# Seven half-size products for the second merge gate, and a changed finish of the attention outputs

## The chip, the cores and the metric

The kernel runs on one core of one Trainium2 chip. A core has a matrix engine (TensorE, PE in the profile), a vector engine (VectorE, DVE), a scalar engine (ScalarE, ACT), a general engine (GpSimd, POOL) and a queue that only issues transfers here (SyncE, SP). Each executes its own list of instructions in order and waits for the others by semaphores. The metric is the device time of one execution in microseconds. Before the change it is 1616.22 us, the median of three runs (1616.01 to 1618.52).

## The reference

One layer of a gated backbone over 1024 latent tokens of width 1024, with 256 context tokens. Both branches start from one input projection of the normalised, modulated input `h`:

```python
p = h @ w_in                       # 11 column groups; the last two are m_gla and m_diff
# branch A: bidirectional chunked gated linear attention -> o_gla
# branch B: differential attention, 8 heads, softmax(q1 k1) - lam * softmax(q2 k2) over 1280 keys -> o_diff
a = merge_heads(rms_norm(o_gla) * gla_gain) * silu(gla_gate)
b = merge_heads(rms_norm(o_diff) * diff_gain * (1 - lam_init)) * silu(diff_gate)
y = sigmoid(m_gla) * (a @ w_br_gla) + sigmoid(m_diff) * (b @ w_br_diff)
x = x + g_x * (y @ w_out)
```

The change touches two things. One is the product that gives `m_diff`, 1024 tokens by 1024 inputs by 1024 channels, called the second merge gate here. The other is what happens to `o_diff` between the attention and the product with `w_br_diff`: the RMS norm over a head's 128 channels and the product with the gate (`diff_gain` and the gate's SiLU are in the stored gate already).

## The kernel before

**Arithmetic.** All large products take fp32 operands as two parts, hi and lo, in a reduced format. `mm3` issues three matmuls for each 128-row piece of the contraction (hi by hi, hi by lo, lo by hi), each with 128 stationary columns and up to 512 moving ones. A weight tile is split by ACT (copy to hi) and DVE (subtraction for lo).

**Order.** The kernel text is written as tasks, Python generators with priorities. When the kernel is built, a planner (`Driver`) runs the tasks against a model of the engines, with costs and latencies, and thereby fixes the order of instructions of every engine. A smaller number is the higher priority. On the chip each engine follows that order.

**Stages.** From 0 to about 890 us: normalisation, projections (four of them by seven half-size products per group, whose input sums `s1` to `s4` are kept in DRAM as `d_s`), and the linear attention. From about 900 to 1440 us: the differential attention, and in it a filler. From 1440 us: `diff`, the product with `w_br_diff`, and the output product.

**The attention.** Its unit is one head and 128 queries; there are 64. For each unit PE computes the scores of two components (12 matmuls into the PSUM tile `s`), DVE takes the maxima (`att_max`), ACT the exponentials (`att_exp`), DVE combines the two (`att_mix`, tile `e`), PE transposes the result in ten pieces (`ident,e`), and `att_split` makes hi and lo: for the first two groups of four pieces ACT copies to `ac` and POOL makes `at` hi and lo, for the last group of two ACT and DVE do it. Two units make a pair; `att_av` multiplies the pair by the values (30 matmuls with 256 columns, `at,vv`). `att_order` fixes the sequence of scores (S), transposes (T) and value products (A), scores some four units ahead of the value products. `att_fin` then finishes a pair: it copies the product, transposes it, forms the norm on ACT, DVE and POOL, multiplies, transposes back and stores to `d_bT`. There are 32 such finishes.

**The filler.** `fill` has the lowest priority (9) and puts its matmuls wherever the attention leaves PE free. It goes through a list: rows 6 and 7 of the first merge gate, the eight rows of the second, and the eight rows of `a @ w_br_gla` ("br"). A row is a weight of 1024 by 128, two slots of `wt` (four in all) for its hi and lo, loaded through `raw` (three slots of 512 KB). It gives two half tiles of 24 matmuls each in the PSUM tile `mb`, of which there is one. A gate's half tile ends in a tanh on ACT (`post`) and a store to `d_m`; a br half tile ends in one operation on DVE and a store to `d_y`. The moving operand of the gates is `hx`, the split input, which fills the 32 slots of `h0` and `h1`; when the gates are done, `d_aT` is loaded there for br. `pace` holds a half tile back until a given attention unit. `presums_a` forms sums of `w_br_diff` on POOL during the attention, in the four slots of `xa`.

**Queues.** All transfers are issued by SP, in the planner's order; a transfer whose source or slot isn't ready holds the ones behind it.

## Time and profile before

| | |
|---|---|
| time of the runs | 1616.22 us median, 1616.01 to 1618.52 |
| profiled execution | span 1614.1 us from first to last instruction; no other time of it is given, and the median lies 2.1 us above its span |
| busy share of the span | PE 99%, PE weight load 82%, DVE 76%, ACT 52%, POOL 39% |
| granted TensorE clock | 1.000 |
| attention and filler | about 900 to 1440 us |
| transfers | 331.16 MB, all compute transfers in one hardware queue |

The page gives totals, a strip of 40 slices, and groups of instructions by engine and operands (`out<-in`, buffer numbers left out). A busy PE is an engine with a matmul in its pipeline: one matmul's duration overlaps that of the next, so what one costs is read from how many fit into a stretch of time, not from its duration.

### The profile page before, as it was taken

The numbers are of one execution on the slowest core, as the hardware profiler recorded it, in microseconds if no ns is written. First come the engines' busy times: TensorE is split into PE (matmuls) and PEld (weight loads), VectorE is DVE, ScalarE is ACT, GpSimd is POOL, SyncE is SP. The second block draws the span as 40 slices with busy tenths as digits, with TensorE's granted clock in tenths as the row PEclk, the third lists the DMA queues.
The fourth block names the chain that finished last, engine by engine and source line by source line (L and its number), as shares of the span: only waits on it lengthen the run. The fifth ranks groups of instructions, "written<-read, shape, count | busy, mean of one in ns | idle before, by whom it ended". The sixth has DMA issues, their size and how long they took to land.

```text
span 1614.1 us, 24349 instructions
## 1 busy us (share of the span) xinstructions
PE 1591.4 (99%) x8229; PEld 1328.1 (82%) x8229; DVE 1224.4 (76%) x2118; ACT 835.7 (52%) x1720; POOL 634.3 (39%) x663
## 2 busy tenths in 40 slices
PE   8999999999999999999999999999999999999999
PEld 3788888888888888888888788888888888888887
DVE  4787945676777779767677688878778888888994
ACT  4776523435343454555535566665665666656331
POOL 1500000001415667535564256656765666560000
PEclk9999999999999999999999999999999999999999
DMA  8576996998878367564645944545587545347662
GB/s 305 201 257 239 329 304 232 344 331 295 278 238 281 116 194 235 167 212 118 189 118 158 253 121 121 151 129 151 150 264 218 159 137 150 111 155 285 204 206 100
DMA packets 259565, 331.16 MB, mean 205 GB/s; under 512 B 22600, under 2 KB 160752, under 8 KB 259440
## 3 DMA queue, kind: packets, MB, share of 16 engines
q1 hardware_dynamic: 259440, 329.60, 63.8%
q8 instruction: 65, 1.06, 0.3%
q14 instruction: 60, 0.49, 0.1%
HBM read 225.20 MB, written 104.33 MB: 204 GB/s over the span
## 4 chain that ended last, share of the span: by engine, by line
PE 89%; DVE 4%; issue 2%; DMA 2%; ACT 1%; POOL 1%; SPq 0%; ACTq 0%; DVEq 0%; POOLq 0%
PE mm L349 30%; PE mb L349 11%; PE s L349 8%; PE mc L349 7%; PE b L349 6%; PE tp L349 5%; PE gt L349 5%; PE b L375 5%; PE go L349 4%; PE gs L349 4%; PE mz L349 2%; PE tp L375 2%; DVE sm L201 1%; POOL at L201 1%; DMA w<-in_w_ada 1%
## 5 line engine op out<-in xcount | busy, mean ns | idle before, releaser
L349 PE MATMUL mm<-w,h 128*128 128x512 f32 x912 | 231.0, 400 | 0.0
L349 PE MATMUL mb<-h,wt 128*128 128x512 f32 x840 | 223.0, 400 | 0.0
L201 DVE TENSOR_REDUCE sm<-s 128x1 f32<-128x1024 f32 (+1 forms) x192 | 193.3, 1037 | 10.7 <-PE s L349 6.6
L201 ACT ACTIVATE e<-s,sm 128x1280 f32<-128x1280 f32 x128 | 169.3, 1329 | 54.4 <-DVE sm L201 51.2
L349 PEld LDWEIGHTS mm<-w,h 128*128 128x128 f32 x912 | 167.4, 188 | 32.8
L201 POOL TENSOR_TENSOR at<-ac,at 128x512 fp32r<-128x512 f32 x128 | 188.2, 1471 | 10.7
L349 PEld LDWEIGHTS mb<-h,wt 128*128 128x128 f32 x840 | 151.4, 188 | 28.6 <-DVE ft L201 0.3
L201 POOL TENSOR_SCALAR at<-ac 128x512 fp32r<-128x512 f32 x128 | 96.9, 757 | 191.0 <-ACT ac L201 190.7
L349 PE MATMUL s<-hk,aq 128*128 128x512 f32 x744 | 169.0, 363 | 1.9 <-ACT e L201 1.8
L349 PE MATMUL mm<-h,w 128*128 128x512 f32 x672 | 168.2, 400 | 1.0 <-DVE h L201 1.0
L349 PEld LDWEIGHTS mm<-h,w 128*128 128x128 f32 x672 | 123.7, 188 | 26.4 <-DVE h L201 1.5
L201 DVE TENSOR_TENSOR w<-raw,w 128x512 fp32r<-128x512 f32 x128 | 96.0, 766 | 54.2 <-ACT w L201 52.0
L349 PEld LDWEIGHTS s<-hk,aq 128*128 128x128 f32 x744 | 117.7, 189 | 18.5 <-ACT e L201 3.6
L349 PE MATMUL b<-at,vv 128*128 128x256 f32 x960 | 130.1, 287 | 1.1 <-ACT ac L201 0.8
L349 PEld LDWEIGHTS b<-at,vv 128*128 128x128 f32 x960 | 119.5, 191 | 2.8 <-ACT ac L201 1.0
L201 ACT ACTIVATE w<-raw 128x512 fp32r<-128x512 f32 x128 | 78.1, 626 | 84.2 <-PE tp L349 23.8
L201 ACT ACTIVATE ac<-b 128x512 f32<-128x512 f32 x122 | 72.5, 598 | 91.8 <-PE b L375 91.7
L201 POOL TENSOR_TENSOR sm<-sm,nhalf 128x2 f32<-128x2 f32 (+2 forms) x94 | 107.7, 1146 | 27.9 <-DVE sm L201 22.7
L201 DVE SCALAR_TENSOR_TENSOR e<-e,sm,e 128x1280 f32<-128x1280 f32 x64 | 117.9, 1842 | 1.0
L349 PE MATMUL mm<-w,g 128*128 128x512 f32 x432 | 105.7, 389 | 0.0
L349 PEld LDWEIGHTS mm<-w,g 128*128 128x128 f32 x432 | 81.1, 188 | 16.9
L375 PE MATMUL b<-ident,e 128*128 128x128 f32 x610 | 92.6, 273 | 1.3 <-ACT ac L201 0.8
(357 smaller groups left out, 3054.2 us busy)
## 6 DMA issues: line engine op xcount, KB each, us to landing
raw<-in_w_in SPq DMA_DIRECT2D x62, 512.0 KB, 4.3
g<-d_s SPq DMA_DIRECT2D x32, 640.0 KB, 6.2
g<-d_s SPq DMA_DIRECT2D x32, 512.0 KB, 5.7
aq<-d_qT SPq DMA_DIRECT2D x124, 128.0 KB, 3.4
d_dv<-pl SPq DMA_DIRECT2D x40, 256.0 KB, 3.9
gv<-d_v SPq DMA_DIRECT2D x40, 256.0 KB, 3.3
d_kT<-pl SPq DMA_DIRECT2D x40, 256.0 KB, 2.8
hk<-d_kT SPq DMA_DIRECT2D x32, 320.0 KB, 5.9
```

What stands on the lines that cost most here:

```text
L201: self.ins = f(out, *args, **kw).ins
L349: self.ins = self.nc.tensor.matmul(out, lhsT, rhs, start=start, stop=stop, skip_group_check=more).ins
L375: self.nc.tensor.transpose(out, src, self.ident[:n, :n])
```

## The change

The second merge gate is computed as a 2 by 2 block product by seven products of half size in every dimension (Winograd's form): `w11`, `w21` and `w22` with parts of the input, and four sums of weight blocks, `t1` to `t4`, with the input sums `s1` to `s4`. The input sums are read from `d_s`. For each of the seven products there are four tiles of 12 matmuls. Two of the products add into the PSUM tile of another (`w21` behind `w11`, `t4` behind `t3`).

The weight blocks are loaded as 512 rows by 256 columns into `raw`, 512 KB each; for `t1` to `t4` one to three more blocks are loaded and added or subtracted on POOL (14 operations of 128x1024). A `wt` slot holds hi and lo of one 512x128 block. Results that are needed again are kept in the four `xa` slots and in four freed slots of `h0` (`u5`), by a copy on ACT or an addition on DVE, and end in a tanh and a store as before. Slots of `h0` and `h1` go to the sums, and then to `d_aT`, piece by piece. `presums_a` starts only when the gate is done (`ev_md`), later than before.

In `att_fin` ACT copies the transposed output out of PSUM and squares it from there, the two small operations on each pair of statistics become one, and the product with the gate and with the norm become one DVE operation per unit. `z` of two units lies in one tile. `PP`, the priority of the fill's results, goes from -1 to -3.5.

```diff
@@ att_scores
+                if qt % 2 == 0:
+                    zp = self.t("sm", [P, 2, 2])
                 u = dict(hd=hd, qt=qt, ...
-                         z=self.t("sm", [P, 2]), left=2, ev=[Event() for _ in range(3)])
+                         z=zp[:, qt % 2], zp=zp, left=2, ev=[Event() for _ in range(3)])
@@
-    PM, PS, PF, PP = -2, -3, -2, -1
+    PM, PS, PF, PP = -2, -3, -2, -3.5
@@ att_fin
-        for x in range(2):
-            self.dve.tensor_scalar(z2[:, x:x + 1], zs[x][:, 0:1], zs[x][:, 0:1], EPS, ALU.mult, ALU.mult)
+        self.dve.scalar_tensor_tensor(z2, zp[:, :, 0], EPS, zp[:, :, 0], ALU.mult, ALU.mult)
...
+        oc = self.t("b1k", [P, 2, P])
+        ss = self.t("sm", [P, 2])
+        self.rel("b1", self.act.activation(oc, pt, AF.Copy))
+        for x in range(2):
+            e = self.act.activation(ot[:, x], oc[:, x], AF.Square, accum_out=ss[:, x:x + 1])
         self.rel("b1k", e)
-        yield On(e, "ACT")
-        oo = self.t("b1k", [P, 2, P])
-        ss = self.t("sm", [P, 2])
+        yield On(e, "DVE")
+        self.dve.scalar_tensor_tensor(ss, ss, 1.0 / P, z2, ALU.mult, ALU.add)
+        yield d.on("POOL", ss)
+        yield On(max(self.pool.tensor_tensor(ss, ss, self.nhalf[:, 0:2], ALU.pow), d.when(g)), "DVE")
         for x in range(2):
-            e = self.act.activation(oo[:, x], pt[:, x], AF.Square, accum_out=ss[:, x:x + 1])
-        yield d.on("DVE", pt, g)
-        e2 = self.dve.tensor_tensor(g, pt, g, ALU.mult)
-        self.rel("b1", max(e, e2))
-        yield On(e, "DVE")
-        for x in range(2):
-            self.dve.tensor_scalar(ss[:, x:x + 1], ss[:, x:x + 1], 1.0 / P, z2[:, x:x + 1], ALU.mult, ALU.add)
-        yield d.on("POOL", ss)
-        yield On(self.pool.tensor_tensor(ss, ss, self.nhalf[:, 0:2], ALU.pow), "DVE")
-        for x in range(2):
-            e = self.dve.tensor_scalar(oo[:, x], g[:, x], ss[:, x:x + 1], None, ALU.mult)
+            e = self.dve.scalar_tensor_tensor(oc[:, x], oc[:, x], ss[:, x:x + 1], g[:, x], ALU.mult, ALU.mult)
@@ fill
-        todo = [(0, s, self.win, C_MG + s * P) for s in range(self.fill_from, 16)] + \
-               [(1, s, a["w_br_gla"][0], s * P) for s in range(8)]
+        OPS = [(n, t) for t in (0, 2) for n in ("w11", "w21")] + [(n, t) for n in ("t2", "t1", "w22") for t in (0, 2)] + \
+              [(n, t) for t in (0, 2) for n in ("t3", "t4")]
+        gates, outs = range(self.fill_from, 8), range(8)
+        todo = [("mg", s) for s in gates] + [("md", n, t) for n, t in OPS] + [("br", s) for s in outs]
+        SUM = dict(t1=("w12", ("w11", ALU.subtract)), t3=("w22", ("w12", ALU.subtract)),
+                   t2=("w11", ("w22", ALU.add), ("w12", ALU.subtract)),
+                   t4=("w21", ("w11", ALU.subtract), ("w22", ALU.subtract), ("w12", ALU.add)))
...
+            for ev, f in parts:
+                yield ev
+                yield d.on("POOL", raw, ev.raw)
+                self.rel("raw", self.pool.tensor_tensor(raw, raw, ev.raw, f))
...
+        h0 = sums("s1") + [("u5",)] + sums("s3") + loads(0, 0, 1, 6, 7) + loads(1, 0, 1, 2, 3)
+        h1 = sums("s2") + sums("s4") + loads(0, 2, 3, 4, 5) + loads(1, 4, 5, 6, 7)
...
+        for t in range(4):
+            yield pace(i)
+            tg, pm = yield from new()
+            yield ev_op["w11", t]
+            yield from product(pm, "w11", t, (0, 0), True, True, copy(pm, X[t], ev_x[t]))
+            i += 0.5
+            yield ev_x[t]
+            e = yield from product(pm, "w21", t, (0, 4), False, True, direct(pm, t, tg))
+            i += 0.5
...
+        for t in range(4):
+            yield pace(i)
+            tg, pm = yield from new()
+            x = ev_u5.x[t]
+            yield from product(pm, "t3", t, "s3", True, True, plus(pm, x, x, ev_z[t], None, gate(x, 1, t, 1, ("h0", 1))))
+            i += 0.5
+            yield ev_z[t]
+            e = yield from product(pm, "t4", t, (1, 4), False, True,
+                                   plus(pm, X[t], X[t], Event(), tg, gate(X[t], 0, t, 1, ("xa", 1))))
+            i += 0.5
+        self.rel("h0", e, 8)
+        self.rel("h1", e, 8)
+        d.set(self.ev_md)
@@ presums_a
         yield self.ev_sb
+        yield self.ev_md
 
         def op(n, k, o, x, y, f, i):
-            yield self.ev_u[min(63, 3*i+9)]
+            yield self.ev_u[min(63, 28 + 2 * i)]
```

The planner's new order shows at three places. The first is PE around the 33rd of the 64 attention units. Before, filler matmuls (`mb<-h,wt`) stand between the scores and the transposes:

```order
L349 MATMUL s_1793_8822<-hk_8707,aq_11661 128x512 x4
L349 MATMUL mb_11875<-h_73_384,wt_11664 128x512
L349 MATMUL mb_11875<-h_74_385,wt_11664 128x512
L349 MATMUL mb_11875<-h_73_384,wt_11665 128x512
L375 MATMUL b_2497_12007<-ident,e_2425_11687 128x128 x4
```

In the changed order, at that place (`mb_11981` is the tile of `t3` and then `t4`, `wt_11677` the weights of `t3`, columns 256 to 383):

```order
L349 MATMUL mb_11981<-h_2317_11089,wt_11677 128x512
L349 MATMUL s_1793_8822<-hk_8707,aq_11612 128x512 x4
L349 MATMUL s_1793_8822<-hk_8707,aq_11612 128x256 x2
L349 MATMUL s_1793_8822<-hk_8707,aq_11615 128x256 x2
...
L349 MATMUL s_1793_8822<-hk_8707,aq_12037 128x512 x4
L375 MATMUL b_2596_12324<-ident,e_2527_12050 128x128 x4
L349 MATMUL mb_11981<-h_192_808,wt_12187 128x512
L349 MATMUL mb_11981<-h_193_809,wt_12187 128x512
L349 MATMUL mb_11981<-h_192_808,wt_12187 128x512
```

Between the last row of `t3` and the first of `t4` no filler matmul stands any more: the rows left out are 48 score matmuls, 42 transposes of `e`, 60 value matmuls and 8 transposes of finishes, less those shown.

The second place is POOL at the same point, where `raw_11738` becomes the weights of `t4` (columns 256 to 511):

```order
L201 TENSOR_TENSOR sm_11924<-sm_11924,nhalf 128x2
L201 TENSOR_TENSOR raw_11738<-raw_11738,raw_11885 128x1024
L201 TENSOR_TENSOR raw_11738<-raw_11738,raw_11910 128x1024
L201 TENSOR_SCALAR at_2517_11976<-ac_12030 128x4x128
L201 TENSOR_TENSOR at_2518_11977<-ac_12030,at_2517_11976 128x4x128
...
L201 TENSOR_TENSOR sm_12124<-sm_12124,nhalf 128x2
L201 TENSOR_TENSOR raw_11738<-raw_11738,raw_12092 128x1024
L201 TENSOR_SCALAR at_2560_12172<-ac_12225 128x4x128
```

Three sums stand among the splits of `at`; four splits (eight rows) are between the second and the third, and what is behind a sum on POOL waits for it. Before, no POOL operation on `raw` exists.

The third is DVE in the first finish of a pair (`b1k`, `sm`). Before:

```order
L201 TENSOR_TENSOR b1k_9201<-b_1881_9213,b1k_9201 128x256
L201 TENSOR_SCALAR sm_9217<-sm_9217,sm_9205 128x1 x2
L201 TENSOR_TENSOR wt_9242<-raw_8854,wt_9241 128x1024
L201 TENSOR_SCALAR b1k_9216<-b1k_9201,sm_9217 128x128 x2
```

and now:

```order
L201 SCALAR_TENSOR_TENSOR sm_9215<-sm_9215,sm_9187 128x2
L201 TENSOR_SCALAR sm_9114<-sm_9114,sm_9112 128x1
L201 TENSOR_REDUCE sm_9229<-s_1793_8822 128x1
L201 SCALAR_TENSOR_TENSOR b1k_9214<-b1k_9214,sm_9215,b1k_9183 128x128 x2
```

The operation that reads PSUM (`b_1881`) is gone from DVE, and the pair of statistics takes one row.

More of the change, by code (lines that the diff above doesn't have):

```diff
@@ L2274, in flush @@
[L2274 to L2286 removed]
+                self.dma(mt, self.d_m[0][s][:, cs])
@@ L2312, in fill @@
-        while n < len(todo):
-            kind = todo[n][0]
-            one = todo[n][:2] in ((1, 6), (1, 7)) or todo[n + 1][0] != kind
-            two = [n] if one else [n, n + 1]
-            end = all(t[0] != kind for t in todo[n + len(two):])
-            for half in range(2):
-                for x in two:
+        i = 0
+        for s in gates:
+            for half in range(2):
+                yield pace(i)
+                e = yield from half_tile(("mg", s), half, self.hx)
+                i += 1
@@ new lines, in copy, with plus, gate @@
+        def copy(pm, x, ev):
+            yield On(0, "ACT")
+            d.set(ev, self.act.activation(x, pm, AF.Copy))
+        def plus(pm, x, y, ev, tg=None, then=None):
+            yield d.on("DVE", y)
+            e = self.dve.tensor_tensor(x, pm, y, ALU.add)
+            if tg:
+                self.rel(tg, e)
+            d.set(ev, e)
+            if then:
+                yield from then
+        def gate(x, c, t, r, *rel):
+            yield d.on("ACT", x)
+            self.act.activation(x, x, AF.Tanh, scale=0.5)
+            self.store([(self.d_m[1][4 * c + t][:, r * 512:(r + 1) * 512], x)], *rel)
@@ L2319, in fill @@
+        self.rel("h0", e, 8)
+        self.rel("h1", e, 8)
+        d.set(self.ev_md)
+        for s0 in range(0, 8, 1):
+            if s0 == 1:
+                continue
+            two = (0, 1) if s0 == 0 else (s0,)
+            for half in range(2):
+                for s in two:
                     yield pace(i)
-                    e = yield from half_tile(x, half, rhs)
+                    e = yield from half_tile(("br", s), half, aT)
                     i += 1
-                if end:
-                    self.rel(f"h{half}", e, 2 * NK)
-                    if half == 0 and kind == 0:
-                        nxt = loads(lambda j, k: self.d_aT[j][k // 2][k % 2], [now] * NK)
```

282 lines of the change are left out of this document (205 added, 77 removed).

## The prediction

> **What bounds the kernel now.** I read the page's totals and the chain of waits first, then two tables by stretches of time (all of PE, and the filler's tile alone), then the timeline of PE in the attention, then the groups of DVE, ACT and POOL.
>
> ```profile
> span 1614.1 us, 24349 instructions
> PE 1591.4 (99%) x8229; PEld 1328.1 (82%) x8229; DVE 1224.4 (76%) x2118; ACT 835.7 (52%) x1720; POOL 634.3 (39%) x663
> PE 89%; DVE 4%; issue 2%; DMA 2%; ACT 1%; POOL 1%; SPq 0%; ACTq 0%; DVEq 0%; POOLq 0%
> ```
>
> PE sets the end: 89% of the chain. The stretches (us; busy, with the count of instructions, of PE, PEld, DVE, ACT, POOL; clock; DMA share; GB/s) show whether its 99% is full. The first and fourth hold nearly only matmuls of 512 columns, the two between are the attention with filler:
>
> ```profile
> 160.00:200.00 40.00, 40.00 (x178) 33.12 (x177) 37.78 (x61) 23.72 (x36) 0.00 (x0) 1.00 0.90 326
> 920.00:1180.00 260.00, 257.66 (x1577) 223.97 (x1576) 214.90 (x397) 162.00 (x332) 165.20 (x145) 1.00 0.52 145
> 1180.00:1440.00 260.00, 258.04 (x1592) 224.72 (x1591) 220.78 (x400) 156.88 (x323) 165.33 (x148) 1.00 0.55 163
> 1520.00:1560.00 40.00, 40.00 (x178) 33.10 (x178) 38.81 (x63) 15.63 (x28) 0.00 (x0) 1.00 0.77 254
> ```
>
> 178 matmuls go into 40 us in stretches 1360 us apart, so one costs 40/178 = 0.225 us, and that is PE's ceiling. In the attention PE is idle for 2.34 + 1.96 = 4.3 us of 520. DVE is at 84% there, POOL at 64%, ACT at 61%. The Trainium skill, Perfetto Trace Analysis, "Identifying the Most-Contended Engine", says that matmul busy time does not tell how near PE is to its limit, and that the weight loads' share does; by it PE has 18% left. The rows disagree as far as "left" goes: 33.1 us of loads in 40 (83%) is what the two full stretches show too.
>
> The timeline of PE (start, us, instruction, count, idle before) gives the price inside the attention:
>
> ```profile
> 1201.05 5.74 PE L349 MATMUL mb<-h,wt 128*128 128x512 f32 x24
> 1206.63 0.38 PE L375 MATMUL b<-ident,b1k 128*128 128x128 f32 x2
> ...
> 1220.05 0.38 PE L375 MATMUL b<-ident,e 128*128 128x128 f32 x2
> ...
> 1223.97 2.41 PE L349 MATMUL b<-at,vv 128*128 128x256 f32 x18 [0.77 <-ACT ac L201]
> ...
> 1229.42 0.95 PE L349 MATMUL mb<-h,wt 128*128 128x512 f32 x3
> ```
>
> 24 filler matmuls take 1206.63 - 1201.05 = 5.58 us, 0.2325 each. The other rows are a stretch without filler, 1220.05 to 1229.42: 9.4 us, in which PE waited 0.77 us.
>
> **The change, part by part.** *Matmuls.* The second gate has 8 rows x 2 halves x 24 = 384 matmuls before, and 7 products x 4 tiles x 12 = 336 after: 48 fewer. At 0.225 to 0.2325 that is 10.8 to 11.2 us; I take -11.0.
>
> *Where they are missing.* By the order PE has as many filler matmuls per unit as before nearly everywhere; but from the last row of `t3` to the first of `t4`, around unit 33, there is none, over 48 scores, 42 transposes and 60 value products. A unit has 12 scores, 10 transposes and 15 value products, so that is 4 units. Before, this place had some 40 filler matmuls. `t4` waits for its weight, a sum of four blocks: three operations on POOL behind three loads that share three `raw` slots. What a unit costs without filler follows from the rows of 920 to 1440 us (62 units):
>
> ```profile
> L201 DVE TENSOR_REDUCE sm<-s 128x1 f32<-128x1024 f32 x122 | 148.3, 1216 | 10.7 <-PE s L349 6.6 <-ACT e L201 3.6
> L201 DVE SCALAR_TENSOR_TENSOR e<-e,sm,e 128x1280 f32<-128x1280 f32 x62 | 114.8, 1852 | 0.9
> L201 DVE TENSOR_REDUCE sm<-s 128x2 f32<-128x512 f32 x61 | 41.5, 680 | 0.0
> L201 DVE TENSOR_SCALAR sm<-sm,sm 128x1 f32<-128x1 f32 x180 | 30.8, 206 | 0.7
> L201 DVE TENSOR_TENSOR at<-b,at 128x256 fp32r<-128x256 f32 x61 | 25.4, 416 | 12.7 <-ACT at L201 12.3
> L201 DVE TENSOR_SCALAR b1k<-b1k,sm 128x128 f32<-128x128 f32 x58 | 24.4, 463 | 28.2 <-POOL sm L201 28.2
> L201 DVE TENSOR_TENSOR wt<-raw,wt 128x1024 fp32r<-128x1024 f32 x16 | 21.5, 1342 | 0.9 <-ACT wt L201 0.9
> L201 DVE TENSOR_SCALAR sm<-sm,sm,nlam 128x1 f32<-128x1 f32 x62 | 16.9, 273 | 2.2
> L201 DVE TENSOR_TENSOR b1k<-b,b1k 128x256 f32<-128x256 f32 x30 | 12.4, 413 | 0.0
> L201 DVE RECIPROCAL sm<-sm 128x1 f32<-128x1 f32 x62 | 9.8, 158 | 24.3 <-ACT e L201 24.1
> L201 DVE TENSOR_SCALAR sm<-sm 128x1 f32<-128x1 f32 x60 | 9.7, 203 | 0.0
> L201 DVE SCALAR_TENSOR_TENSOR ft<-ft,mb 128x512 f32<-128x512 f32 x14 | 9.5, 682 | 5.9 <-PE mb L349 5.9
> L349 PE MATMUL mb<-h,wt 128*128 128x512 f32 x768 | 205.4, 401 | 0.0
> ```
>
> PE: 515.7 us busy, less 771 filler matmuls (these and 3 in `mc`) at 0.2325 = 179, leaves 336, or 5.4 us a unit. DVE: the two maxima, the mix, `at`, `nlam` and the reciprocal are 356.7 us / 62 = 5.75, and two minima at 0.206 make 6.2 us a unit; a finish (half a one per unit) adds to it, below. So a unit without filler is set by DVE, not by PE: with 0.65 for the finish 6.8 us, and four units 27.3 against PE's 21.6. The scores run some four units ahead, so PE can live on what stands ready. Bounds for the idle time: 0.77/9.4 of 21.6, that is 1.8 us, as in the short stretch above; or all of DVE's excess, 5.7 us. POOL may be worse:
>
> ```profile
> L201 POOL TENSOR_TENSOR at<-ac,at 128x512 fp32r<-128x512 f32 x128 | 188.2, 1471 | 10.7
> L201 POOL TENSOR_SCALAR at<-ac 128x512 fp32r<-128x512 f32 x128 | 96.9, 757 | 191.0 <-ACT ac L201 190.7
> L201 POOL TENSOR_TENSOR sm<-sm,nhalf 128x2 f32<-128x2 f32 x34 | 31.8, 936 | 22.9 <-DVE sm L201 22.7
> L201 POOL TENSOR_TENSOR xa<-xa,xa x16: 1283/1920/2548, 973.1 to 1348.5; 128x512 f32<-128x512 f32 x16
> ```
>
> The sums (128x1024) do not exist before; twice the `xa` sums' shortest, median and longest is 2.6, 3.8 and 5.1 us. I take 3.8. Two splits of 2.23 and half a power make 4.9 us a unit, four units 19.7, with three sums 31.2: 9.6 us more than PE. But two of the three stand at the head of the stretch, where POOL still has slack. Between 1.8, 5.7 and 9.6 I take 4.5, nearest to DVE's.
>
> *The other eleven sums* (42 us) stand in units 8 to 31, where 9 of the 16 `xa` sums (17 us) leave for later: POOL goes from 165 to 190 of 260 us, 73%. It stays covered, but splits behind a sum come later, and A waits for them:
>
> ```profile
> PE s L349 <- ACT e L201: 2.0, 3, 1.3
> PE b L375 <- DVE b1k L201: 1.8, 4, 0.7
> PE b L349 <- POOL at L201: 0.3, 1, 0.3
> ```
>
> 16 `xa` sums left 0.3 us of waiting for POOL. For longer ones I take 1.0, between 0 and 4 us (0.37 for each of eleven). The Trainium skill, GPSIMD Engine Reference, "Engine selection", speaks against this edit: elementwise work on two inputs belongs on VectorE, and the section on the reconciled numbers gives 4497 ns for 2048 fp32 elements, by which a sum would be 2.25 us (an estimate) and the 14 some 31 us; then the 1.0 would be nearly 0. The trace's shortest `xa` sum, 1.283 for 512, lies above the 1.12 that this gives, so the measurement decides.
>
> *DVE* gains and loses. A finish costs 2 x 0.206 + 2 x 0.463 + 0.413 + 2 x 0.203 = 2.16 us before; after, two pair operations at 0.2 and two scalings, which I price at the 0.463 of those they replace, 1.33. 32 of them: -26.6. Weight splits go from 17 of 1024 columns to 9, and 28 of 512 are added: 28 x 0.67 (half of 1.342) less 8 x 1.342 = +8.0. 20 additions out of PSUM at the 0.682 of `ft`: +13.6. Sum -5 us of 436: hidden below PE.
>
> *ACT* gets 32 more copies of 128x256, 12 more half splits, 4 copies:
>
> ```profile
> L201 ACT ACTIVATE b1k<-b 128x256 f32<-128x256 f32 x64 | 24.8, 388 | 30.8 <-PE b L375 25.2 <-PE b L349 5.2
> L201 ACT ACTIVATE wt<-raw 128x1024 fp32r<-128x1024 f32 x17 | 18.2, 1070 | 0.0
> L201 ACT ACTIVATE ft<-mb 128x512 f32<-128x512 f32 x20 | 12.1, 606 | 4.3 <-PE mb L349 3.6 <-DMA aq<-d_qT 0.7
> ```
>
> 32 x 0.388 + 28 x 0.535 - 8 x 1.07 + 4 x 0.606 = 21 us: 319 becomes 340 of 520, 65%, covered by PE. The chain of a finish stays about as long (a copy is added on ACT, DVE's product goes), while its PSUM slot comes free sooner. Of the 1.8 us that PE waited for finishes (`DVE b1k`) up to all may go, and as much may come, since the copy stands ahead of the squares: 0.
>
> *Transfers*: 52 more issues on SP: 32 sums of 256 KB (8.4 MB) and 20 more weight blocks of 512 KB (10.5 MB), 19 MB, in the 260 us whose DMA share is 0.52 at 145 GB/s: +73 GB/s, a share near 0.8. Stretch 160 to 200 moved 326 GB/s with PE full. I add nothing, up to 1.5 us.
>
> Sum: -11.0 + 4.5 + 1.0 = -5.5. The profiled execution's span of 1614.1 becomes 1608.6; the median of the runs lies 2.1 above that span, and I keep this: **1610.7 us**.
>
> **Rivals.** *The gap is covered*: the four units run on what was ahead, idle 1.8, nothing else is late: 1616.2 - 11.0 + 1.8 = 1607.0. For it: 0.77 us in 9.4 us without filler. Against: that stretch was one unit long.
>
> *The gap takes all*: POOL sets it, 9.6 us, and the rest costs 1: 1615.8, no change. For it: two sums right ahead of four splits. Against: 191 us of idle time on POOL.
>
> *PE isn't the limit*: it has room, its matmuls are only paced by DVE's results, fewer of them make more room, and the end stays, 1616. Against: 178 matmuls in 40 us with DVE at 37.8 or 38.8 us and ACT at 23.7 or 15.6. This is what the share of the weight loads on the page named above, Perfetto Trace Analysis of the Trainium skill, would give.
>
> *Slower: POOL holds up the value products.* Each of 14 sums makes the splits behind it late, and A, in PE's fixed order, holds scores and filler behind it. With the gap at 4.5, from (11.0 - 4.5 + 3.2)/14 = 0.7 us of PE waiting for each sum this decides; at 1.2, half of what 3.8 exceeds a split's 1.47, it is 17: 1616.2 - 6.5 + 17 = 1626.5. For it: POOL is in order. Against: 0.3 us lost to 16 sums of 1.9 us, and the planner has placed the value products behind the splits with sums in between.
>
> **How the numbers follow.** Forecast 0.50 (own range 1607.5 to 1613.5), covered 0.14, takes all 0.18, not the limit 0.05, slower 0.13. What a measurement of this kernel can tell from no change is 0.2%, 3.2 us: faster means below 1613.0, slower above 1619.5. Faster: nearly all of the forecast (0.47) and the covered case, 0.61. Same: 0.18 + 0.05 + 0.03 and a little of the slower case, 0.27. Slower 0.12. The range leaves out the slower case and the edge below: 1605.5 to 1617.0.
>
> **What would show it.** Right: 48 matmuls fewer in `mb`; a PE wait of 2 to 9 us at the first matmuls of `t4` from column 256 on, or spread over the attention's matmuls in the four units before; `raw` sums near 3.8 us; DVE below 84%; the end 5 to 6 us earlier. Wrong: PE waits for POOL `at` of many us (the slower case), no idle time in the gap (covered), `raw` sums near 2.3 us or above 5, or a change in the stages before 890 or after 1480 us, where the instructions are the same.

## The result: slower, and the profile after

The change makes the kernel slower: 1654.15 us median (1651.66 to 1656.84, four runs) against 1617.37 (1616.01 to 1619.80) before, a ratio of 1.0226 with a 95% interval of 1.021 to 1.0241. That is 36.8 us more, where I had forecast 5.5 us less and a range of 1605.5 to 1617.0. Two of the later kernels (`sums_alone` and `fewer_and_no_low`) had one run each in a slower state, which their times leave out.

The page of the changed kernel begins with the totals (busy us, share of the span, instructions), and its chain of waits shows what ended last:

```profile
span 1655.1 us, 24385 instructions
PE 1599.5 (97%) x8181; PEld 1328.5 (80%) x8181; DVE 1275.3 (77%) x2062; ACT 860.4 (52%) x1776; POOL 674.7 (41%) x677
PE 78%; DVE 9%; issue 4%; POOL 3%; DMA 3%; ACT 2%; SPq 0%; ACTq 0%; POOLq 0%; DVEq 0%
```

PE has exactly the 48 matmuls fewer (8229 to 8181), yet it is busy 8 us longer. PE's share of the chain falls from 89% to 78%, DVE's rises from 4% to 9%. DVE is busy 50.9 us longer (1224.4 before), with 56 instructions fewer.

The table by stretches, with the columns as in the prediction, says where:

```profile
160.00:200.00 40.00, 40.00 (x177) 32.81 (x177) 37.98 (x61) 25.18 (x39) 0.00 (x0) 1.00 0.87 312
920.00:1180.00 260.00, 241.74 (x1419) 204.43 (x1417) 230.75 (x353) 163.79 (x336) 170.90 (x138) 0.98 0.67 194
1180.00:1440.00 260.00, 244.84 (x1484) 211.38 (x1482) 223.28 (x350) 158.33 (x326) 177.31 (x151) 0.98 0.61 176
```

The early stretch is as before. In the attention PE is now idle for 18.3 + 15.2 = 33.4 us of 520, where it was 4.3, and its clock is 0.98 in place of 1.00. DVE is at 87%, where I expected less than 84%. The waits of PE in the attention (880 to 1500 us; what waited for what, us in total, times, longest) are spread over many places:

```profile
PE b L375 <- DVE b1k L201: 8.8, 11, 2.0
PE s L349 <- ACT e L201: 5.4, 9, 1.8
PE b L375 <- DVE sm L201: 4.4, 3, 2.0
PE b L375 <- DVE at L201: 3.2, 6, 0.8
...
PE mb L349 <- DVE ft L201: 2.8, 1, 2.8
PE mb L349 <- DVE xa L201: 2.6, 3, 1.3
```

Five of these six name DVE: the finish (`b1k`), the last group's split (`at`), a result of br (`ft<-ft,mb`, at 1255 us) and the products' additions (`xa`). In the three waits for `sm` a small operation of the softmax had just ended, but DVE's `at` split, which reads a `b` tile and frees it, had ended 0.15 us before each of these transposes too; so `sm` may stand for `at`. POOL's `at`, which my slower rival would have made the largest, has 1.3 us.

DVE's groups in the attention (900 to 1480 us; busy us, mean ns of one) show what grew:

```profile
L201 DVE SCALAR_TENSOR_TENSOR b1k<-b1k,sm,b1k 128x128 f32<-128x128 f32 x60 | 47.0, 823 | 8.2 <-POOL sm L201 8.2
L201 DVE TENSOR_TENSOR wt<-raw,wt 128x512 fp32r<-128x512 f32 x30 | 31.3, 1046 | 0.2 <-ACT wt L201 0.2
L201 DVE SCALAR_TENSOR_TENSOR sm<-sm 128x2 f32<-128x2 f32 x31 | 24.0, 776 | 0.0
L201 DVE TENSOR_TENSOR wt<-raw,wt 128x1024 fp32r<-128x1024 f32 x9 | 11.6, 1284 | 0.0
L201 DVE SCALAR_TENSOR_TENSOR sm<-sm,sm 128x2 f32<-128x2 f32 x30 | 10.8, 359 | 0.0
L201 DVE TENSOR_TENSOR xa<-mb,xa 128x512 f32<-128x512 f32 x8 | 5.5, 682 | 0.1
```

A finish now costs DVE 2 x 0.823 + 0.776 + 0.359 = 2.78 us. It was 2.16, and I had forecast 1.33: +19.9 us for 32 of them in place of -26.6. A half-size split costs 1.046 in place of 0.67: 28 x 1.046 + 11.6 less 17 x 1.335 is +18.2 in place of +8.0. Only the additions out of PSUM came as forecast, 20 x 0.68 = +13.6. The sum is +51.7, the 50.9 of the totals.

The timeline shows one such stall (start, us, engine, operation, count, idle before):

```profile
1172.29 4.81 POOL L201 TENSOR_TENSOR raw<-raw,raw 128x1024 f32<-128x1024 f32 x2
1172.60 4.65 DVE L201 SCALAR_TENSOR_TENSOR b1k<-b1k,sm,b1k 128x128 f32<-128x128 f32 x2
...
1177.30 0.44 PE L375 MATMUL b<-ident,b1k 128*128 128x128 f32 x1 [2.02 <-DVE b1k L201]
1177.40 2.05 PE L349 MATMUL s<-hk,aq 128*128 128x512 f32 x4
```

Two sums run on POOL from 1172.29 to 1177.10. Two DVE operations on 128 columns take 4.65 us meanwhile, a transpose waits 2.02 us for them, and then four score matmuls take 2.05 us, which take 1.09 at other places. The last step is the clock. Around this stall, and around another at 983 us, the stretches of 3.41 us read:

```profile
982.83:986.23 3.40, 1.40 (x10) 0.95 (x9) 3.40 (x7) 0.22 (x1) 0.29 (x1) 1.00 0.60 169
986.23:989.64 3.41, 3.41 (x12) 2.73 (x10) 2.71 (x5) 3.41 (x6) 2.26 (x3) 0.50 0.31 103
1173.97:1177.38 3.41, 0.85 (x6) 0.48 (x6) 3.41 (x3) 0.00 (x0) 3.05 (x2) 1.00 0.44 103
1177.38:1180.79 3.41, 3.41 (x13) 2.92 (x14) 3.41 (x6) 1.27 (x3) 0.00 (x0) 0.50 0.85 271
```

In the first of each pair PE works 1.40 and 0.85 us of 3.4, and DVE is busy for all of it; in the second the granted clock is 0.50. The mean clock of the whole run is 0.991, against 1.000 before. At half clock PE loses half of a stretch, so 0.009 x 1655 = 15 us is the most that this can have cost. It is part of how a stall is paid, not what starts it: `old_finish`, below, has a clock of 0.998 and is 32.3 us slower than before all the same.

### The profile page after: what moved, and what is told of

It is laid out like the page before. It is cut to its first block, busy times and chain, and to the rows that moved or that the text cites. A ratio compares the mean times of both kernels' runs of the same rounds, so it can differ in the third digit from the quotient of the medians.

```text
span 1655.1 us, 24385 instructions
## 1 busy us (share of the span) xinstructions
PE 1599.5 (97%) x8181; PEld 1328.5 (80%) x8181; DVE 1275.3 (77%) x2062; ACT 860.4 (52%) x1776; POOL 674.7 (41%) x677
## 4 chain that ended last, share of the span: by engine, by line
PE 78%; DVE 9%; issue 4%; POOL 3%; DMA 3%; ACT 2%; SPq 0%; ACTq 0%; POOLq 0%; DVEq 0%
PE mm L349 29%; PE mb L349 7%; PE mc L349 7%; PE s L349 6%; PE tp L349 5%; PE gt L349 4%; DVE sm L201 4%; PE b L349 4%; PE go L349 4%; PE gs L349 4%; PE b L375 3%; POOL at L201 2%; PE tp L375 2%; PE mz L349 2%; DVE e L201 1%
## 5 line engine op out<-in xcount | busy, mean ns | idle before, releaser
L349 PE MATMUL mb<-h,wt 128*128 128x512 f32 x792 | 214.1, 406 | 5.9 <-DVE ft L201 2.8
L201 DVE TENSOR_REDUCE sm<-s 128x1 f32<-128x1024 f32 (+1 forms) x192 | 193.7, 1036 | 18.3 <-PE s L349 16.8
L201 POOL TENSOR_TENSOR at<-ac,at 128x512 fp32r<-128x512 f32 x128 | 195.7, 1529 | 10.7
L349 PE MATMUL s<-hk,aq 128*128 128x512 f32 x744 | 175.1, 370 | 7.6 <-ACT e L201 5.1
L349 PEld LDWEIGHTS mb<-h,wt 128*128 128x128 f32 x792 | 144.2, 192 | 33.8 <-DVE xa L201 3.6
L349 PEld LDWEIGHTS s<-hk,aq 128*128 128x128 f32 x744 | 120.1, 193 | 26.5 <-ACT e L201 9.1
L375 PEld LDWEIGHTS b<-ident,e 128*128 128x128 f32 x608 | 75.1, 142 | 29.5 <-issue 7.7
```

Of the source, the lines that this page charges most:

```text
L201: self.ins = f(out, *args, **kw).ins
L349: self.ins = self.nc.tensor.matmul(out, lhsT, rhs, start=start, stop=stop, skip_group_check=more).ins
L375: self.nc.tensor.transpose(out, src, self.ident[:n, :n])
```

## The experiments

Eighteen kernels ran. Differences below are to the runs of the kernel before on the same chip, so the change itself stands at +36.8. Its 95% interval reaches 2.5 us to each side, and those of the other kernels 1.5 to 4 us, so a difference between two of them is known to some 3 us.

One more thing limits what they show. `no_sums`, `no_sums_no_loads`, `no_low` and the last three kernels keep the written order, since `d.op` enters an operation in the plan and issues none. In all other kernels of the layer the planner made a new order. `true_costs`, the same instructions in another order, took 5.8 us more than the change; so differences of this size there can come from the order alone.

### The finish alone, and the products alone

The first pair parts the change. `old_finish` is the changed kernel with the finish of before:

```diff
-    def att_fin(self, hd, pr, po, zp):
+    def att_fin(self, hd, pr, po, zs):
...
-        self.rel("b1", self.act.activation(oc, pt, AF.Copy))
...
+        e2 = self.dve.tensor_tensor(g, pt, g, ALU.mult)
```

> The changed kernel with the finish of the attention outputs as it was before; the seven products, the input sums and the priority stay. Theory A (DVE operations with two SBUF tensors as inputs stand still while POOL works, and the new finish has four of them where the old one had none): the finish's DVE time falls from 82 us to about 61, and the rows behind it come in time; 1618 to 1632 us. Theory B (the seven products leave PE without filler and with waits of their own, whatever the finish does): 1645 to 1655 us.

Measured: 1650.46 us, ratio 1.0198 (1.0183 to 1.0214), +32.3. Theory A falls: the finish isn't what costs most. DVE is as busy (1274.8 us) as with the new finish: the old finish's scalings, with one SBUF tensor each, take 0.640 us here, against 0.288 beside an idle POOL (below). `new_finish` is the kernel before with the new finish alone, the same difference the other way round:

> The kernel before with the new finish alone, no seven products. Theory A: slower by the DVE time that the finish gains and the waits behind it, 1628 to 1647 us, with the scalings b1k at 0.6 to 0.8 us instead of 0.29. Theory B: the finish is not at fault, 1611 to 1619 us.

Measured: 1622.67 us, ratio 1.0028 (1.0019 to 1.0038), +4.5, between the ranges of the two theories. Both pairs put the finish at 4.5 us and the products at some 32, but 4.5 is within what a new order can do. DVE is busy 1240.8 us in this kernel, 16.4 more than before, and without any sums on POOL.

`finish_psum` leaves the finish's copy out and lets the last operation read PSUM, which holds a bank of `b1` longer:

```diff
-        self.rel("b1", self.act.activation(oc, pt, AF.Copy))
...
-            e = self.act.activation(ot[:, x], oc[:, x], AF.Square, accum_out=ss[:, x:x + 1])
+            e = self.act.activation(ot[:, x], pt[:, x], AF.Square, accum_out=ss[:, x:x + 1])
...
-            e = self.dve.scalar_tensor_tensor(oc[:, x], oc[:, x], ss[:, x:x + 1], g[:, x], ALU.mult, ALU.mult)
+            e = self.dve.scalar_tensor_tensor(oc[:, x], pt[:, x], ss[:, x:x + 1], g[:, x], ALU.mult, ALU.mult)
+        self.rel("b1", e)
```

> The changed kernel, but the last operation of the finish reads the transposed product from PSUM; no copy on ACT, the squares read PSUM as before. The scaling then has one SBUF tensor as input instead of two. Theory A: b1k scalings near 0.3 us, 1612 to 1630 us. Theory B: 1643 to 1655 us.

Measured: 1676.38 us, ratio 1.0352 (1.0333 to 1.0371), +58.2. That lies above both theories: DVE gets lighter (1243.0 us busy in place of 1275.3) and the kernel 21 us slower. PE's largest waits there are for ACT's `ac` (11.8 us) and DVE's `ft` (10.6). That the longer hold of the PSUM slot is the cause wasn't tested by itself; the order is new as well.

### What an operation on DVE costs beside POOL

Two small kernels, which aren't the layer, time DVE's forms beside POOL. In the first the forms follow each other in turn:

> Not the layer: only a list of DVE operations, eight rounds of seven forms, with POOL idle, then beside a row of POOL operations with two inputs (128x1024), then beside POOL operations with one input (128x512). Theory A: the forms with two SBUF tensors (128x128, 128x2, 128x512) take 1.5 us and more beside two-input POOL operations, the forms with an input in PSUM stay within 10% of the idle price. Theory B: every form stays within 10% of its idle price.

Its scaling of 128x128, with one SBUF tensor (`idle` with POOL idle, `two` beside POOL's two-input operations):

```profile
L55 DVE TENSOR_SCALAR twots<-fg,sc 128x128 f32<-128x128 f32 x8 | 17.3, 2160 | 0.0
L55 DVE TENSOR_SCALAR idlets<-fg,sc 128x128 f32<-128x128 f32 x8 | 2.3, 288 | 0.0
```

The form with two tensors took 352 and 651 ns; with an input in PSUM it took 354 and 339. But in a round of seven forms the scaling bore nearly all of the waiting, and the 128x512 form with two SBUF inputs, two places behind it, took 679 ns beside POOL as well. So the price of the other forms was not settled. The second kernel gives each form its own block:

> Not the layer: eight DVE operations of one form in a row, each form in a block of its own, first with POOL idle, then with POOL doing 128x1024 two-input operations back to back. If two SBUF inputs on both sides share one access path in turn, the 128x512 subtraction with both inputs in SBUF goes from about 0.69 to 1.0-1.4 us and the 128x128 two-input operation from 0.35 to 0.6-0.7; with one input in PSUM the 128x512 and 128x1024 stay at 0.68 and 1.2; the 128x2 operations rise from 0.15 to 0.7 or more, since in the changed kernel they took 0.776.

Its groups on DVE; names that begin with `idle` are with POOL idle, with `two` beside POOL's 128x1024 operations (2408 ns each):

```profile
L50 DVE TENSOR_TENSOR twotts<-fg,fh 128x512 f32<-128x512 f32 x8 | 19.7, 2457 | 0.2
L56 DVE SCALAR_TENSOR_TENSOR twostts<-fg,sc,fh 128x128 f32<-128x128 f32 x8 | 18.1, 2263 | 0.2
L58 DVE SCALAR_TENSOR_TENSOR twosmall<-sc 128x2 f32<-128x2 f32 x8 | 9.4, 1173 | 0.2
L50 DVE TENSOR_TENSOR idletts<-fg,fh 128x512 f32<-128x512 f32 x8 | 5.5, 692 | 0.2
L52 DVE TENSOR_TENSOR twottp<-pm,fh 128x512 f32<-128x512 f32 x8 | 5.5, 689 | 0.2
L56 DVE SCALAR_TENSOR_TENSOR idlestts<-fg,sc,fh 128x128 f32<-128x128 f32 x8 | 2.8, 351 | 0.2
L58 DVE SCALAR_TENSOR_TENSOR idlesmall<-sc 128x2 f32<-128x2 f32 x8 | 1.3, 160 | 0.2
```

With both inputs in SBUF, 128x512 goes from 692 to 2457 ns and 128x128 from 351 to 2263: about one DVE operation for each POOL operation, whatever its own size. With one input in PSUM 128x512 stays at 689. As the 679 ns above shows, not every such operation waits. I had expected 1.0 to 1.4 us for the 128x512: the price is worse than sharing in turn. The Trainium skill, SBUF — State Buffer, "Who interferes with whom", says just this: an instruction with two SBUF inputs contends with a GpSimd instruction that reads SBUF, the one that starts first holds the shared path for its whole length, and one with at most one SBUF input isn't touched outside the modes that use both ports, which `tensor_scalar` can enter. The rows of the second kernel agree; the scaling's 2160 ns in the first would fit such a mode, but no row tells it. This fits the groups of the changed kernel: its splits, scalings and pair operations read SBUF alone and are longer, its additions have an input in PSUM and are not.

### The sums

`no_sums` leaves out the 14 sums on POOL and keeps the order of everything else (`d.op` enters an operation in the plan and issues none); the second gate is computed from the first block of each sum alone:

```diff
-                self.rel("raw", self.pool.tensor_tensor(raw, raw, ev.raw, f))
+                self.rel("raw", d.op("POOL", 0.14 + 0.00216 * 1024, [raw], [raw, ev.raw]))
```

> The changed kernel without the 14 additions and subtractions on POOL (128x1024, 2.65 us each, 37.1 us in all); all 28 blocks are still loaded, the order on every other engine is the same, and the products run on the first block alone, so the second gate is not the reference's. Theory S, the sums are what costs (they hold DVE's SBUF operations, whose 128x512 `wt` subtraction went from 680 to 1046 ns, and they come late, so that ACT waits on `wt` behind POOL): the time falls from 1654 to 1618-1630, and the mean of the `wt` subtraction to below 800 ns. Theory W, the smaller pieces cost (28 half-size splits, 20 DVE additions from PSUM and one `mb` bank between products): it stays at 1645-1655. In between (1632-1643) both hold about half.

Measured: 1645.42 us, ratio 1.0165 (1.0149 to 1.018), +26.5: the sums are worth 10.3 of the 36.8 us. Theory S isn't enough, and of W most is left. DVE is busy 13.5 us less (1261.8). The half-size `wt` splits went from 1046 to 959 ns only; POOL's splits of `at`, which read SBUF too, remain. `no_sums_no_loads` adds to this that the 14 extra blocks aren't loaded:

```diff
-                        d.set(ev, self.dma(ev.raw, block(n0, x[2])))
+                        d.set(ev, d.dma(4 * P * 1024, ev.raw, block(n0, x[2])))
```

> As the kernel without the sums (1645.4), and the 14 blocks that only the sums read are not loaded either (7.3 MB less): same order otherwise, the gate is not the reference's. If the transfers (the queues' share rose from about 0.5 to 0.72-0.82) hold something up, by late landings or by keeping raw slots from the next weight: 1630-1640. If they are hidden: 1643-1647.

Measured: 1644.18 us, ratio 1.0162 (1.0139 to 1.0185), +26.4, in the range for hidden transfers. The other way round, `sums_alone` puts 14 POOL operations of the sums' shape into the kernel before:

```diff
+            if kind == 0 and s >= 8:
+                for x in range(2 if s < 14 else 1):
+                    yield d.on("POOL", raw)
+                    self.pool.tensor_tensor(raw, raw, raw, ALU.mult)
```

> The kernel before with 14 POOL multiplications of the same shape (128x1024, raw by itself) put in front of the eight weight splits of its second gate (two ahead of six of them, one ahead of two); its gate is then not the reference's. Theory S: 1617 rises to 1635-1650, with DVE's SBUF operations longer and ACT waiting on POOL. Theory W: 1617-1623.

Measured: 1630.94 us, ratio 1.0073 (1.0051 to 1.0096), +12.0, between the two theories and of the size that `no_sums` gave, though these operations, with one tile as both inputs, take 1.98 us each in place of 2.65. DVE is busy only 6 us longer there (1230.3), while PE's wait for finishes (`DVE b1k`) rises from 1.8 to 7.2 us. The powers (`sm<-sm,nhalf`), which a finish waits for, also stand in POOL's queue; but only one of the 32 follows right behind a sum, so how the sums delay the finishes isn't shown.

### DVE's work in the products

`no_low` leaves out DVE's 28 half-size splits; the high part stands in for the low one, the order stays:

```diff
-                    e = self.dve.tensor_tensor(w[:, 1], r, w[:, 0].bitcast(F32), ALU.subtract)
+                    e = d.op("DVE", 0.07 + 512 * 0.00104, [w[:, 1]], [r, w[:, 0]])
```

> The changed kernel without DVE's 28 `wt` subtractions of the seven products (about 1.05 us each, 29 us in all); the products use the high part of the weight in place of the low one, so the gate is not the reference's, and the order and the number of matmuls stay. Theory D (DVE has too much to do from 960 to 1320 us, and everything that PE waits for there stands behind it): 1654 falls to 1622-1638. Theory L (latency: one `mb` bank, drains and sums between half-size products, whatever DVE's load): it stays at 1645-1656.

Measured: 1645.99 us, ratio 1.0173 (1.0156 to 1.019), +28.2: 29 us of DVE time are worth 8.6. By my own bounds this speaks for L, but it isn't nothing. `act_drain` replaces the 20 additions by copies on ACT, so nothing is added:

```diff
-            yield d.on("DVE", y)
-            e = self.dve.tensor_tensor(x, pm, y, ALU.add)
+            yield d.on("ACT", y)
+            e = self.act.activation(x, pm, AF.Copy)
```

> The changed kernel with DVE's 20 additions from PSUM (0.68 us each, 13.6 us) replaced by copies from PSUM on ACT into the same tiles; nothing is added, so the gate is not the reference's. Theory D (what stands in DVE's queue is what costs, and the drain in it holds the one `mb` bank): 1654 falls to 1636-1644. Theory L (the bank is drained between products 28 times whatever engine does it): 1650-1656.

Measured: 1640.38 us, ratio 1.0134 (1.0117 to 1.0151), +22.1, as D had it. Without the additions on DVE the kernel is 14.7 us faster, the largest single part, though they are only 13.6 us of DVE's work. Not all of it need be theirs: the order is new, and the mean clock of the profiled run is 0.997 in place of 0.991. `copy_then_add` keeps the result and parts the two things: ACT copies the product and frees the bank, DVE adds from SBUF:

```diff
-            e = self.dve.tensor_tensor(x, pm, y, ALU.add)
-            if tg:
-                self.rel(tg, e)
+            e = self.act.activation(c, pm, AF.Copy)
+            if tg:
+                self.rel(tg, e)
+            yield d.on("DVE", c)
+            e = self.dve.tensor_tensor(x, c, y, ALU.add)
```

> The changed kernel with each of the 20 additions parted in two: ACT copies the product from PSUM and frees the bank, then DVE adds from SBUF; the same result. If the drain's place in DVE's queue costs (the bank waits there): 1640-1648. If DVE's load does (its 20 additions stay and read two SBUF inputs): 1652-1664.

Measured: 1650.14 us, ratio 1.0202 (1.0187 to 1.0218), +31.9, between the two cases. With the bank freed early the kernel is 4.9 us faster, and the additions on DVE, now with two SBUF inputs, keep the other 9.8. That suggests mostly DVE's load and partly the bank, but 4.9 us is also what a new order can do. `gate_by_dve` tests the same in the kernel before, whose 16 gate outputs are taken out of PSUM by DVE:

```diff
-                self.rel(tg, self.act.activation(mt, pm, AF.Tanh, scale=0.5))
+                    self.rel(tg, self.dve.tensor_scalar(mt, pm, 1.0, 0.0, ALU.mult, ALU.add))
+                    yield d.on("ACT", mt)
+                    self.act.activation(mt, mt, AF.Tanh, scale=0.5)
```

> The kernel before, with the 16 outputs of its second gate taken out of PSUM by DVE (128x512, about 0.68 us each, 10.9 us in all) and the tanh done in place by ACT: the same result. It is the DVE drain of the changed kernel without products, sums or pieces. Theory D: 1617 rises by 6 to 12, to 1623-1629. Theory L: by 0 to 4.

Measured: 1630.69 us, ratio 1.0082 (1.0067 to 1.0097), +12.9 for 10.9 us of operations, a little above what D gave. One wait there is `PE mb <- DVE wt` of 3.1 us: the filler itself now stands behind DVE.

### The written order

`post_late` puts the priority of the products' finish operations back (`PP` from -3.5 to -1):

> The changed kernel with the priority of the fill's finish operations put back from -3.5 to -1 (the planner then issues the product's copies and additions after the attention's own work). If the early place of the products' drains ahead of the attention's softmax and finish work is what costs: 1630-1642. If the drains' lateness would then hold the one `mb` bank: 1655-1675.

Measured: 1654.16 us, ratio 1.0219 (1.0199 to 1.0239): no difference to the change, and neither of my two cases. `true_costs` gives the planner, in the attention, prices nearer to those measured (0.4 us more for DVE's `wt` and `b1k` operations out of SBUF, 0.35 for the pairs, 2.55 ns for each element on POOL):

> The changed kernel with the planner's prices in the attention set nearer to what the trace shows (POOL two-input operation 0.14 + 2.55 ns per element in place of 2.16; on DVE 0.4 us more for each `wt` and `b1k` operation that reads SBUF alone, 0.35 us more for the small `sm` pairs); same instructions, another order. If a plan made with too low prices is at fault (it puts work on the path because it thinks that a neighbour is done): 1625-1640. If the resources themselves are short (DVE about 90% busy from 960 to 1320 us): 1648-1660.

Measured: 1661.52 us, ratio 1.026 (1.0239 to 1.0282), +42.6, above both cases. An order made with prices nearer to the measured ones is no better, so nothing here points to the planner's prices as the cause.

### All of it at once, and what 48 matmuls are worth

`all_relief` combines them: no sums, no half-size low parts, additions as copies on ACT, the old finish. What is left of the change is the 28 small products and their loads.

> The changed kernel without the POOL sums, without the 28 low-part subtractions, with the 20 additions as ACT copies and with the finish of the kernel before; the planner is told, the gate is not the reference's. What is left of the change is 28 products of 12 matmuls in place of 16 of 24 and the input loads. If sums, DVE work and finish are the whole of the loss: 1606-1614. If half-size products with a drain between them lose by themselves: 1622-1635.

Measured: 1626.89 us, ratio 1.0055 (1.004 to 1.007), +8.6, inside my second case. The four parts win 28.2 us together, less than their sum of 10.3 + 8.6 + 14.7 + 4.5 = 38.1; that they relieve the same queue would explain it and isn't shown. One stretch of the kernel before, then two of this one and two of its waits:

```profile
920.00:1400.00 480.00, 476.04 (x2919) 414.45 (x2918) 398.80 (x735) 292.38 (x600) 303.68 (x268) 1.00 0.55 159
920.00:1400.00 480.00, 473.13 (x2877) 406.90 (x2875) 386.05 (x722) 309.36 (x637) 299.92 (x269) 1.00 0.68 201
1400.00:1480.00 80.00, 70.64 (x414) 60.60 (x413) 59.32 (x115) 42.87 (x96) 36.90 (x36) 0.94 0.37 118
PE mc L349 <- ACT wt L201: 3.6, 1, 3.6
PE mc L349 <- DVE wt L201: 1.5, 1, 1.5
```

Up to 1400 us PE is busy nearly as long as before (2.9 us less in 480), but it gets through 42 matmuls fewer in that time (2877 against 2919), at a clock of 1.00: by the count it is already behind, which its busy time hides. Then it is idle for 9.4 of 80 us, and the next products (`mc`) wait for their weights. The order of this kernel was made anew, and its last value product starts at 1463.9 us against 1452.5 before; what makes the attention 11 us late is open.

`48_fewer` asks for the first term of the prediction by itself. It is the kernel before, all in the same order, without the last of the eight input blocks in the 16 half tiles of the second gate:

```diff
+                N = NK - 1 if kind == 0 and s >= 8 else NK
+                if k < N:
...
+                else:
+                    for _ in range(3):
+                        e = x[1] = d.op("PE", 0.009 + 512 * 0.000428, [pm], [hi, lo])
```

> The kernel before with 48 matmuls left out of its second gate (the last of the eight input blocks in all 16 half tiles, so the gate is not the reference's), all else in the same order. If PE's own work sets the attention's pace, as the prediction's first term has it: 1617.8 falls by 9 to 11, to 1607-1609. If the chain through DVE, ACT and POOL is as long as PE's work there: by 0 to 5, to 1613-1618.

Measured: 1615.68 us, ratio 0.9985 (0.9975 to 0.9994), -2.6 us with an interval of -4.0 to -1.0, inside the second case. The stretch that holds most of the 48, in the kernel before and in this one, and the exponentials of all heads (count; ns of one; first and last start) in both:

```profile
910.00:1250.00 340.00, 335.58 (x2038) 291.36 (x2039) 277.37 (x507) 208.89 (x424) 210.53 (x186) 1.00 0.59 170
L201 ACT ACTIVATE e<-s,sm x128: 1318/1330/1348, 904.2 to 1427.4; 128x1280 f32<-128x1280 f32 x128
```

```profile
910.00:1250.00 340.00, 329.57 (x2003) 283.21 (x2001) 282.27 (x511) 208.73 (x424) 210.20 (x186) 1.00 0.59 172
L201 ACT ACTIVATE e<-s,sm x128: 1315/1329/1341, 906.1 to 1426.7; 128x1280 f32<-128x1280 f32 x128
PE b L375 <- DVE b1k L201: 5.3, 9, 0.9
PE s L349 <- ACT e L201: 3.2, 5, 1.3
```

PE is busy 6.0 us less in the same 340 us, and the exponentials take 520.6 us in place of 523.2. What PE doesn't do it waits: for `b1k` 5.3 us in place of 1.8, for `e` 3.2 in place of 2.0. The last pair takes DVE's load away, with and without the 48 matmuls (in the second gate's eight full splits):

```diff
+                if todo[n][0] == 0 and todo[n][1] >= 8:
+                    e = d.op("DVE", 0.07 + 1024 * 0.00104, [lo[:, ks]], [raw[:, ks], hi[:, ks]])
```

> The kernel before with 48 matmuls fewer, as before (1615.7), and also without DVE's eight 128x1024 low-part subtractions of the second gate (1.335 us each, 10.7 us; the high part stands in for the low one, the gate is not the reference's), all else in the same order. If the chain through DVE is the other limit, which kept 48 matmuls from being worth 11 us: 1606-1611. If what holds the attention is neither PE's work nor DVE's load but the latencies of its chains in the written order: 1613-1616.

> The control: the kernel before without those eight subtractions alone, all its matmuls kept. PE is 99% busy in the attention, so DVE's relief alone should give 0 to 3 us: 1615-1618. A fall to below 1613 would mean that DVE, and not PE, set the pace before.

Measured: 1612.64 us, ratio 0.9961 (0.9947 to 0.9975), -5.8, with both, between my two cases; 1616.29, ratio 0.9984 (0.9975 to 0.9993), -2.1, without DVE's 10.7 us alone, as expected. Within the noise the gains add up, 2.6 + 2.1 against 5.8, and each alone is a quarter or a fifth of the work taken away. So neither PE's work nor DVE's load alone sets the attention's pace; that the latencies of its chains in the written order do is what is left, and isn't shown by itself.

None of the kernels that compute the whole layer was faster than the kernel before.

## Why the prediction was wrong

**The first step failed**: "PE sets the end", and so "-11.0" for 48 matmuls. The count was right, the price was 2.6 us. I took PE's ceiling from two stretches that hold only matmuls and found PE 99% busy in the attention; that shows how seldom PE has no matmul in it, not that it gives time back when it has less. The rival "PE isn't the limit", at 0.05, was right on this step, and what I held against it came from other stages. The rule of the Trainium skill, Perfetto Trace Analysis, "Identifying the Most-Contended Engine", I had set aside with the same rows; `48_fewer` agrees that PE had room, without showing that the share of the weight loads measures it.

**DVE, "-5 us, hidden"**, was wrong in sign, size and cover. Measured +50.9. The two scalings that I "price at the 0.463 of those they replace" cost 0.823, the pair operations that I put at 0.2 cost 0.776 and 0.359, the half splits 1.046 in place of 0.67. I carried durations over from operations with other operands, beside a POOL that had no sums. And the cover that I named, PE, was the thing that waited: in the two stalls shown DVE is busy all the time.

**The additions, +13.6 on DVE**, were right in size, but costed at nothing on the path. `act_drain` puts them at up to 14.7 us, and `gate_by_dve`, with 16 such drains in the kernel before, at 12.9: each stands in DVE's queue and holds the one `mb` bank until its turn.

**The sums.** At 2.65 us each (2.34 to 3.64, most of them 2.4) they are shorter than my 3.8. The gap without filler around unit 33 was there, from 1172.90 to 1202.96 us; the second row is the same gap, in the same order, in `no_sums`:

```profile
1172.90:1202.96 30.06, 25.08 (x152) 21.90 (x150) 27.10 (x39) 17.79 (x40) 22.10 (x15) 0.89 0.68 175
1166.18:1192.48 26.30, 23.12 (x151) 20.50 (x150) 23.11 (x39) 17.92 (x40) 14.67 (x12) 0.94 0.57 141
```

PE is idle for 30.06 - 25.08 = 5.0 us of it; the forecast was 4.5. Without the sums it is idle for 3.2 us, waiting for the softmax and DVE's `at`, so my reading of a unit without filler holds in part; but that the sizes agree is luck, since in the changed kernel 2.6 us of the 5.0 are waits for `b1k`, 2.0 of them the stall shown above, which I hadn't in the sum, and the clock of 0.89 comes on top. The sums cost 30.06 - 26.30 = 3.8 us here. "The other eleven sums ... 1.0" failed: all 14 are worth 10.3, so about 6.5 outside the gap. They don't act mainly through POOL's `at` (1.3 us of waits, with and without them), as my slower rival had it; DVE, which they hold, is busy 13.5 us longer with them. That rival had the right sign and the wrong place.

**The finish chain, 0**: measured 4.5, not clear of the order, with DVE 16 us busier where I had it 27 less busy. **Transfers, 0**: right, by `no_sums_no_loads`. **ACT, hidden**: its copies came as forecast (0.385 us), its half splits at 0.636 in place of 0.535, and it is busy for 62% of the attention, where I had 65%. What the terms leave, 8.6 us in `all_relief`, is open.

The slower outcome had 0.13, all of it on one mechanism. It should have had more: the change took work off an engine whose saving was unproven and put three kinds of work on DVE's queue and one beside it on POOL.

## What to carry to other kernels

An engine that is 99% busy with filler isn't therefore the one whose work is worth removing: take the work out in the same order and see, before paying for its removal elsewhere. Price an added DVE operation by where its operands lie and by what POOL does at that time: with two SBUF inputs it can last as long as POOL's whole operation (2457 ns in place of 692), and so can a scaling with one (2160 in place of 288); with an input in PSUM it kept its own time. Draining the only bank on a busy engine cost more than the operation itself, 12.9 us for 10.9 us of work, so try it on the engine whose queue is shortest.

## What the runs showed of the hardware that I had not expected

A DVE operation on two columns took 1173 ns in place of 160, and one on 128 columns 2263 in place of 351, when POOL worked with two inputs beside it.

PE's clock halved after a stretch of 3.41 us in which PE was partly busy, 1.40 and 0.85 us of it, with no single wait above 2.02 us at those two places. The Trainium skill, TensorE: Matmul & The Clock Gate, "What's actually happening", has the lower clock after at least one idle window of about 3.4 us; here the windows have that length, but a window that was 25% or 41% busy was enough. Two more windows of the changed kernel:

```profile
1057.91:1061.33 3.42, 1.62 (x10) 1.06 (x9) 3.42 (x9) 1.91 (x4) 3.25 (x4) 1.00 0.94 323
1249.06:1252.47 3.41, 1.84 (x14) 1.40 (x13) 2.49 (x4) 2.89 (x6) 3.41 (x3) 1.00 1.00 243
```

Behind the first the clock halved, behind the second it didn't. On this grid, from 60 to 1600 us, it halved after all seven windows in which PE was busy for 0.6 to 1.62 us, and after none with 1.84 us or more. The border isn't the same in every run: in `act_drain` a window with 1.57 us, at 1504.5, left the clock at 1.00.
